# Gated attention: the next tile's low-rank transposition right behind the sums of decays, its gates' product one group sooner, and the sampled decays' sums in one bank

## The chip, the core and the metric

The kernel runs on one core of one Trainium2 chip. The metric is the device time of one launch in microseconds (us), lower is better. Besides the engines' own names, PE is TensorE, DVE is VectorE, ACT is ScalarE, POOL is GpSimd and SP is SyncE, whose queue issues the DMAs.

## The reference

One layer of a decoder: 2048 prompt tokens and 64 sampled tokens pass an input projection, sliding-window attention and gated linear attention side by side, an output projection and an MLP. The change touches the gated linear attention alone. Cut to that part, for 4 heads with keys of 64 and values of 128:

```python
log_a = jax.nn.log_sigmoid(glr @ w_gk2 + b_gk) / 16.0      # glr: 16 columns of the projection, the low-rank gate
b = cumsum(log_a) within a chunk                           # sums of decays
k_rel = exp(where(causal, b_t - b_s, -inf)) * k_s
o = (q_t . k_rel) v_s  +  (q * exp(b)) S                   # inside the chunk, and from the state
S = exp(b_last) * S + (k * exp(b_last - b))^T v            # the state that is carried on
out = rms_norm(o, g_gla) * silu(gr)
```

## The kernel before

The program runs in stages: attention, then the gated attention, then the output projection and the MLP. In the stage of the gated attention (some 430 us of the span) the 2048 prompt tokens are 16 tiles of 128 (`NB = 16`). Tile 16 (`i == NB`) is the 64 sampled tokens, whose own recurrence `gla_sample` is woven in between as `side`.

Tensor work of two kinds is interleaved on PE by hand. The *filling* is the generator `products()`: the input projections of tiles 16, 2, 3, ... 15 (tiles 0 and 1 were projected before), each in four chunks of columns in the order `G_ORDER = (3, 0, 1, 2)`, 24 products a chunk. Chunk 3 holds the 16 low-rank columns. The *recurrence* is `gla(i)`, a generator that yields the number of filling products to put behind its step. For a tile it issues:

1. `qk_T` (tile `gqk`): transposed queries and keys, then 38 filling products (`G_FILL[0]`) and the transposition `ogT` of the previous tile's output, whose copy out on ACT is `mo`, L1046.
2. `es`: the sums of decays from a position to the tile's end, two products into a bank of kind "d". ACT takes their exponential into `kd` (L1077). Then the output gate (`gate`, tile `sg`), the levels of decays, and 14 filling products.
3. Four groups of products `gm` (levels 0 and 1, 2 and 3, 4 and 5, then 6), 9 filling products between them. Behind each group stands one step of `decayed(i + 1)`, the preparation of the next tile: behind the first group `pg`, the transposition of the 16 low-rank columns, which DVE copies to `glrT` (L934); behind the second `z`, their product with the gate's weights, from which ACT and DVE make the logarithms `zt` (L940 to L943); behind the third `tT`, their transposition, copied to `before` (L1058), from which the levels of the next tile are summed (`level_sums`, L998 to L1003).
4. `ds`, 13 filling products, `o` (the output) and `finish_out` up to its yield.

Accumulators are banks by kind: kinds "a", "b" and "c" have two buffers each, "d" and "e" one. `gqk`, `es`, `pg`, `z` and `ds` all use the one bank "d", so each must wait until what the one before left there has been read. Projections take the two "a" in turn.

Engines run their instructions in the order in which the framework placed them. On PE that is the order of the code; on DVE and ACT the framework's scheduler mixes the steps, so one moved step can move others.

## Time and profile before

| what | value |
|---|---|
| median of 3 runs | 2268.26 us (2267.26 to 2268.97) |
| the profiled execution | 2265.7 us, its span 2263.9 us |
| mean granted TensorE clock | 0.993 |
| PE busy in the span | 2200.4 us (97%) |
| DVE, ACT, POOL busy in the span | 1620.4, 1203.7, 271.1 us |
| stage of the gated attention, 342 to 770 us: PE, DVE, ACT busy | 412.5, 358.6, 216.8 us of 428.0 |

The span runs from the first to the last instruction; 1.8 us lie around it. A row of the timeline gives start, length, engine, line, instruction, output<-inputs and count, and in brackets the time that the engine sat idle before it and what ended it. The small matmuls of PE overlap: a projection product is listed with some 0.35 us but starts 0.18 us after the one before. Almost all tensor instructions are listed under L140, a helper's line, so they are told apart by the tile that they write.

### The profile page before, as it was taken

What the parts mean: (1) busy time and instruction counts of PE and PEld (TensorE: products, weight loads), DVE (VectorE), ACT (ScalarE), POOL (GpSimd) and SP (SyncE); (2) the same over time, 40 slices, a digit from 0 to 9 for tenths busy, and PEclk for the clock granted to TensorE, in tenths of its full rate; (3) what the DMA queues carried; (4) which work ended last, traced back from release to release, by engine and by line L of the source; (5) the groups of instructions that cost most, each with busy time, mean ns of one, the idle gap of its engine ahead of it and who ended that gap; (6) DMA issues with size and microseconds to landing.
All of it is one profiled execution on the core that took longest, in us unless ns stands there. A gap on an engine that the chain in (4) does not pass through costs nothing.

```text
span 2263.9 us, 34089 instructions
## 1 busy us (share of the span) xinstructions
PE 2200.4 (97%) x11800; PEld 1879.6 (83%) x11800; DVE 1620.4 (72%) x3365; ACT 1203.7 (53%) x2498; POOL 271.1 (12%) x426
## 2 busy tenths in 40 slices
PE   8999999999999999999999999999999999999997
PEld 7888888889988788878888878888888888888886
DVE  5888878888888776687767787878544645755557
ACT  5777764445555444555555655555444444554445
POOL 2566412112121110000000000000000000000000
PEclk9999999999999999999999999999999999999999
DMA  7344222121112455865555666666655755866665
GB/s 235 119 140 143 96 88 77 58 73 52 62 52 66 144 190 182 274 212 206 183 186 201 251 219 213 228 245 229 226 184 178 228 175 185 279 226 216 223 194 197
DMA packets 229938, 392.65 MB, mean 173 GB/s; under 512 B 23057, under 2 KB 137638, under 8 KB 225782
## 3 DMA queue, kind: packets, MB, share of 16 engines
q1 hardware_dynamic: 229766, 390.48, 51.3%
q8 instruction: 93, 1.52, 0.3%
q14 instruction: 79, 0.65, 0.1%
HBM read 255.61 MB, written 135.86 MB: 173 GB/s over the span
## 4 chain that ended last, share of the span: by engine, by line
PE 70%; DVE 17%; ACT 6%; issue 3%; DMA 3%; POOL 1%; SPq 0%; DVEq 0%; ACTq 0%; POOLq 0%
PE dn L140 23%; PE uc L140 7%; PE ua L140 7%; PE gproj L140 7%; PE out L1266 6%; PE ud L140 3%; PE ue L140 3%; PE ub L140 3%; DVE s L140 2%; PE proj L140 2%; DVE AT L1009 1%; PE sam L140 1%; PE dsam L140 1%; PE out L140 1%; DVE pl L140 1%
## 5 line engine op out<-in xcount | busy, mean ns | idle before, releaser
L140 PE MATMUL dn<-ot,os 128*128 128x512 f32 x2688 | 623.6, 390 | 3.8 <-DVE ot L140 1.9
L140 PEld LDWEIGHTS dn<-ot,os 128*128 128x128 f32 x2688 | 503.9, 188 | 112.9 <-DVE ot L140 5.4
L140 DVE TENSOR_TENSOR os<-os 128x512 fp32r<-128x512 f32 x224 | 154.9, 691 | 228.4 <-ACT os L140 228.0
L140 ACT ACTIVATE os<-os 128x512 fp32r<-128x512 f32 x224 | 141.4, 631 | 280.9 <-DMA os<-s_d 233.0
L140 PE MATMUL gproj<-wg,gx 128*128 128x384 f32 (+1 forms) x1408 | 279.4, 348 | 1.9 <-ACT s_dec L612 1.6
L140 PEld LDWEIGHTS gproj<-wg,gx 128*128 128x128 f32 x1408 | 246.8, 191 | 12.4 <-issue 10.1
L140 ACT ACTIVATE st<-st 128x512 f32<-128x512 f32 x225 | 142.1, 632 | 135.3 <-DVE st L140 131.2
L140 PE MATMUL uc<-H,s 128*128 128x512 f32 x744 | 180.4, 392 | 3.4 <-ACT st L140 3.4
L140 PE MATMUL ua<-H,w 128*128 128x512 f32 x744 | 179.2, 390 | 0.6 <-ACT st L140 0.6
L140 PEld LDWEIGHTS uc<-H,s 128*128 128x128 f32 x744 | 140.7, 189 | 33.2 <-ACT st L140 3.9
L140 PEld LDWEIGHTS ua<-H,w 128*128 128x128 f32 x744 | 138.7, 188 | 28.9 <-ACT st L140 0.8
L216 POOL TENSOR_TENSOR frs<-rs_v,half 128x1 f32<-128x1 f32 (+1 forms) x13 | 8.8, 680 | 1235.0 <-DVE rs_v L140 1235.0
L140 DVE TENSOR_TENSOR st<-st 128x512 f32<-128x512 f32 x160 | 110.5, 692 | 61.9 <-ACT st L140 58.7
L1266 PE MATMUL out<-wo,mt 128*128 128x512 f32 x608 | 141.5, 391 | 0.0
L1266 PEld LDWEIGHTS out<-wo,mt 128*128 128x128 f32 x608 | 113.2, 188 | 22.9
L140 DVE TENSOR_TENSOR ot<-ot 128x512 fp32r<-128x512 f32 x128 | 88.4, 690 | 13.9 <-ACT ot L140 13.4
L140 ACT ACTIVATE s<-t 128x1024 fp32r<-128x1024 f32 x62 | 65.8, 1061 | 58.1 <-PE ue L140 24.6
L140 PE MATMUL proj<-wa_hi,xh 128*128 128x384 f32 (+1 forms) x272 | 95.7, 355 | 0.9 <-ACT wa_hi L140 0.6
L140 PE MATMUL proj<-wa_lo,xh 128*128 128x384 f32 (+1 forms) x272 | 94.3, 351 | 0.0
L140 PE MATMUL proj<-wa_hi,xl 128*128 128x384 f32 (+1 forms) x272 | 93.3, 347 | 0.0
L140 DVE TENSOR_TENSOR s<-t,s 128x1024 fp32r<-128x1024 f32 x62 | 76.0, 1226 | 21.7 <-ACT s L140 18.6
L140 ACT ACTIVATE ot<-ot 128x512 fp32r<-128x512 f32 x128 | 80.8, 631 | 19.6 <-DMA ot<-t_d 18.0
(407 smaller groups left out, 4107.9 us busy)
## 6 DMA issues: line engine op xcount, KB each, us to landing
os<-s_d SPq DMA_DIRECT2D x224, 256.0 KB, 2.8
s_d<-st SPq DMA_DIRECT2D x31, 1792.0 KB, 8.4
raw<-in_w_up SPq DMA_DIRECT2D x64, 512.0 KB, 5.7
ot<-t_d SPq DMA_DIRECT2D x128, 256.0 KB, 3.3
rt<-in_w_down SPq DMA_DIRECT2D x96, 256.0 KB, 3.0
t<-in_w_down SPq DMA_DIRECT2D x64, 256.0 KB, 3.3
t_d<-t SPq DMA_DIRECT2D x32, 512.0 KB, 6.9
gx<-xt_d SPq DMA_DIRECT2D x28, 512.0 KB, 4.1
```

What stands on the lines that cost most here:

```text
L140: ins = call(*a, **k)
L216: nc.gpsimd.tensor_tensor(out, v[:n], e, op=ALU.pow)
L1009: nc.vector.copy_predicated(dst, m, gm.rearrange("p h (m b) -> p h m b", b=b))
L1266: te.matmul(p_, x, w[:, cc], start=k + u == 0, stop=k == KT - 1 and u == len(products) - 1)
```

## The change

Four edits:

1. The steps of `decayed(i + 1)` are started right behind `es` of tile `i`, if chunk 3 of the next tile has been projected by then (`ahead`). `pg` so stands between `es` and the 14 filling products, and its next step, `z`, behind the first group of `gm` instead of the second. Behind the second group then stands nothing, and `tT` stays behind the third. By the order of the built program `ahead` holds in tiles 0 to 12; in tiles 13 and 14 the steps stand where they stood.
2. The projection's chunk 1 of the sampled tokens (tile 16) is summed in bank "e" instead of "a".
3. The sampled tokens' sums of decays for both pairs of heads go into one bank, and one exponential takes them instead of two.
4. `decayed` fetches its projection itself.

```diff
-            p_ = bank([P, 512], "a", f"gproj_{i}_{c}")
+            p_ = bank([P, 512], "ae"[(i, c) == (NB, G_ORDER[2])], f"gproj_{i}_{c}")
...
     def gla(i, gp, og=iter(())):
...
+        following = decayed(i + 1) if i < NB - 1 else iter(())
         next(og, None)
...
         ex = nc.scalar.activation(kd, e_, AF.Exp, scale=1.0 / 16)
         nc.gpsimd.tensor_tensor(kd, kd, gp[:, 256:512], op=ALU.mult)
+        ahead = (i + 1, 3) in projected
+        if ahead:
+            next(following, None)
         with tc.issue_after(ex.ins):
             sg = gate(i, gp, P)
...
-        following = decayed(i + 1, gps[i + 1]) if i < NB - 1 else iter(())
...
-            next(following, None)
+            if not (ahead and l0 == 2):
+                next(following, None)
...
+        e_ = bank([P, 2, (SL + 1) * NS], "b", "se")
         for g in range(2):
-            e_ = bank([P, (SL + 1) * NS], "b", f"se_{g}")
-            te.matmul(e_, lh[:NS, g * P : (g + 1) * P], slev, start=True, stop=False)
-            te.matmul(e_, ll[:NS, g * P : (g + 1) * P], slev, start=False, stop=True)
-            nc.scalar.activation(s_dec[:, g].rearrange("p l t -> p (l t)"), e_, AF.Exp, scale=1.0 / 16)
+            te.matmul(e_[:, g], lh[:NS, g * P : (g + 1) * P], slev, start=True, stop=False)
+            te.matmul(e_[:, g], ll[:NS, g * P : (g + 1) * P], slev, start=False, stop=True)
+        nc.scalar.activation(s_dec.rearrange("p g l t -> p g (l t)"), e_, AF.Exp, scale=1.0 / 16)
```

The first place is PE in tile 6, between the sums of decays and the second group. `gproj` are filling products. Before:

```order
L140 MATMUL es_6891<-lh_4955,c_suf 128x256
L140 MATMUL es_6891<-ll_4957,c_suf 128x256
L140 MATMUL gproj_1_6879<-wg_1_4344,gx_7_6496 128x384
...
L140 MATMUL gm_0_6969<-XQ,qk_4950 64x2x32 x4
L140 MATMUL gm_0_6969<-XQ,XK 64x2x32 x4
L140 MATMUL pg_6978<-ident,gp_6851 16x128
...
L140 MATMUL gm_2_6996<-XQ,XK 64x2x32 x8
L140 MATMUL z_7005<-wgk,glrT_4935 128x256
```

and in the change:

```order
L140 MATMUL es_6889<-lh_4955,c_suf 128x256
L140 MATMUL es_6889<-ll_4957,c_suf 128x256
L140 MATMUL pg_6894<-ident,gp_6849 16x128
L140 MATMUL gproj_1_6877<-wg_1_4344,gx_7_6494 128x384
...
L140 MATMUL gm_0_6970<-XQ,qk_4950 64x2x32 x4
L140 MATMUL gm_0_6970<-XQ,XK 64x2x32 x4
L140 MATMUL z_6979<-wgk,glrT_4935 128x256
...
L140 MATMUL gm_2_7002<-XQ,XK 64x2x32 x8
```

`pg` moved ahead of the 14 filling products and of the first group, directly behind `es`; `z` moved ahead of 9 filling products and of the second group.

The second place is DVE in tile 9. The names: `before` and L1003 are the sums of the levels, the one written 128x2x64 is the last; `XK` and `XQ` are keys and queries times their decays, `rs_v` and `og` belong to the previous tile's output. Before:

```order
L971 COPY qk_4951<-gqk_7653 128x2x128
L1002 TENSOR_TENSOR after_4949<-after_4949,before_4948 128x4x32
...
L214 TENSOR_SCALAR rs_v<-ossq_7639 128x4
...
L1031 SCALAR_TENSOR_TENSOR og_4939<-o_7632,ors_7645,sg_4943 128x128 x4
...
L1003 TENSOR_TENSOR before_4948<-before_4948 128x4x32
...
L1003 TENSOR_TENSOR before_4948<-before_4948 128x2x64
```

and in the change:

```order
L1003 TENSOR_TENSOR before_4948<-before_4948 128x4x32
L1017 COPY_PREDICATED AT<-dmsk,dg_7722 128x512
L971 COPY qk_4951<-gqk_7651 128x2x128
L1003 TENSOR_TENSOR before_4948<-before_4948 128x2x64
...
L214 TENSOR_SCALAR rs_v<-ossq_7637 128x4
...
L1031 SCALAR_TENSOR_TENSOR og_4939<-o_7630,ors_7643,sg_4943 128x128 x4
```

The last two sums moved from behind `og` to ahead of it. So it is in tiles 3 to 8 before and in tiles 2 to 11 and 13 in the change; in tiles 1, 2 and 9 to 14 before, and in tiles 1, 12 and 14 in the change, the last sum stands behind `og`.

The third place is DVE in tile 6, around the copy of `pg` and the logarithms. Before:

```order
L1090 TENSOR_TENSOR qd_4945<-qk_4950,dec_4947 128x256
L956 SCALAR_TENSOR_TENSOR sg_4943<-gp_6574,sg_4943 128x512
L1009 COPY_PREDICATED AT<-c_1527,gm_0_6969 64x4x32
L934 COPY glrT_4935<-pg_6978 16x128
...
L1009 COPY_PREDICATED AT<-c_1527,gm_2_6996 64x4x4x8 x2
L943 SCALAR_TENSOR_TENSOR zt_4952<-z_7005,zt_4952 128x256
```

and in the change:

```order
L1093 TENSOR_TENSOR qd_4945<-qk_4950,dec_4947 128x256
L934 COPY glrT_4935<-pg_6894 16x128
L956 SCALAR_TENSOR_TENSOR sg_4943<-gp_6572,sg_4943 128x512
L1009 COPY_PREDICATED AT<-c_1527,gm_0_6970 64x4x32 x2
L1009 COPY_PREDICATED AT<-c_1527,gm_0_6970 64x4x16x2 x2
L943 SCALAR_TENSOR_TENSOR zt_4952<-z_6979,zt_4952 128x256
```

The copy moved ahead of the gate and of the first group's copies, and the logarithms' last step ahead of the second group's.

## The prediction

> **What bounds the kernel now.** I read the page first: PE is busy 97% of the span, DVE 72%, ACT 53%. The change touches only the stage of the gated attention, so I then asked for that stage's waits of PE. A row names who waits, for whom, the sum in us, how often, and the longest.

> ```profile
> PE z L140 <- DVE glrT L934: 4.8, 7, 2.1
> PE tT L140 <- DVE zt L943: 3.1, 3, 1.4
> PE gm L140 <- DVE AT L1009: 2.7, 2, 2.4
> PE gproj L140 <- ACT s_dec L612: 1.6, 1, 1.6
> PE se L140 <- ACT s_qk L972: 1.1, 1, 1.1
> PE pg L140 <- ACT kd L1077: 0.6, 2, 0.3
> ```

> Some 14 us of waits in a stage of 428 us: PE is the bound almost everywhere, and the change aims at four of these six rows. Even if all of them went, the kernel would gain 0.6%. Any new wait on PE, on the other hand, is paid in full. So I cut the stage into tiles, from the second `es` product of one tile to that of the next. The columns are the stretch, its length, and PE's busy time in it (count, clock and DMA follow).

> ```profile
> 477.68:504.65 26.97, 25.23 (x197) 1.00 0.34 104
> 504.65:528.02 23.37, 23.37 (x182) 1.00 0.17 57
> 528.02:551.41 23.39, 23.39 (x181) 1.00 0.17 58
> ...
> 598.29:622.08 23.79, 23.45 (x182) 1.00 0.17 57
> 622.08:646.64 24.56, 23.58 (x181) 1.00 0.15 54
> 646.64:670.56 23.92, 23.52 (x182) 1.00 0.16 57
> 670.56:695.07 24.51, 23.61 (x181) 1.00 0.16 54
> 695.07:719.44 24.37, 23.56 (x181) 1.00 0.15 42
> ```

> The first row is tile 4. Tiles 5 and 6 are full: 23.37 us of work in 23.37 us. Tiles 9 to 13 lose 0.42, 1.19, 0.55, 1.14 and 1.00 us against that, 4.3 us together.

> **Part 1: `pg` right behind `es`.** Both use the one bank "d", so `pg` must wait until ACT has read the sums of decays (`kd`, L1077). Before, 14 filling products and a group lay between them. Tile 6, PE and then ACT:

> ```profile
> 528.02 0.27 PE L140 MATMUL es<-ll,c_suf 128*128 128x256 f32 x1
> 528.13 2.59 PE L140 MATMUL gproj<-wg,gx 128*128 128x384 f32 x14
> ...
> 531.27 0.28 PE L140 MATMUL pg<-ident,gp 128*16 128x128 f32 x1
> 531.30 1.83 PE L140 MATMUL gproj<-wg,gx 128*128 128x384 f32 x9
> ```

> ```profile
> 528.10 0.60 ACT L1046 ACTIVATE mo<-ogT 128x512 f32<-128x512 f32 x1 [0.55 <-PE ogT L140]
> 528.59 0.38 ACT L1077 ACTIVATE kd<-es 128x256 f32<-128x256 f32 x1
> ```

> `kd` cannot start at once: ACT first copies `ogT`, which PE finished just ahead of `es`. It ends at 528.97, when PE before had been in the filling for 0.84 us. What a waiting `pg` does to PE is seen in tile 10, where ACT was so late that `pg` waited in spite of its distance:

> ```profile
> 624.47 0.42 ACT L1088 ACTIVATE dec<-before 128x256 f32<-128x256 f32 x1 [4.18 <-DVE before L1003]
> ...
> 625.27 0.38 ACT L1077 ACTIVATE kd<-es 128x256 f32<-128x256 f32 x1
> ```

> ```profile
> 625.70 0.28 PE L140 MATMUL pg<-ident,gp 128*16 128x128 f32 x1 [0.30 <-ACT kd L1077]
> 625.74 1.83 PE L140 MATMUL gproj<-wg,gx 128*128 128x384 f32 x9
> ...
> 628.73 0.69 PE L140 MATMUL z<-wgk,glrT 17*128 17x256 f32 x2 [0.54 <-DVE glrT L934]
> ```

> PE stood still until 0.05 us after the end of `kd` (625.65), and the filling behind went on 0.04 later: nothing overtakes a waiting `pg`. So in tile 6 the filling would start at 528.97 + 0.09 = 529.06 instead of 528.13, less 0.03 for the slot of `pg` that is no longer spent at 531.27: 0.90 us lost. Queued behind it are the 14 filling products, `gm`, and with `gm` DVE. A tile of this kind has no idle time on PE that could give it back. The DVE order puts the last sums ahead of `og` in tiles 2 to 11 of the change, the pattern of tile 6 (`kd` on time): 10 x 0.90 = 9.0 us. (Bounds 0.7, if the copy `mo` starts sooner, to 1.0.)

> Tile 12 has its last sum behind `og`, as tiles 9 to 14 had before. There ACT waits for that sum (the 4.18 us above) with `mo` and `kd` queued behind. Where the filling began behind `es` in tiles 9 and 12, and what ended the wait:

> ```profile
> 598.40 2.59 PE L140 MATMUL gproj<-wg,gx 128*128 128x384 f32 x14
> ...
> 670.67 2.59 PE L140 MATMUL gproj<-wg,gx 128*128 128x384 f32 x14
> ...
> 674.13 0.28 PE L140 MATMUL pg<-ident,gp 128*16 128x128 f32 x1 [0.25 <-ACT kd L1077]
> ```

> ```profile
> 600.30 0.38 ACT L1077 ACTIVATE kd<-es 128x256 f32<-128x256 f32 x1
> ```

> As in tile 9 (the first of its row to be late, as tile 12 will be) the loss is 600.68 + 0.09 - 598.40 - 0.03 = 2.3 us, as in tile 12 674.13 - 670.67 = 3.5. I take the middle, 2.9.

> Tiles 0 and 1 are different: there the sampled tokens' work keeps DVE nearly full (first row: stretch, length, DVE busy), and PE's end of tile 0 waits for DVE's `og`.

> ```profile
> 358.43:385.85 27.42, 25.37 (x72) 0.94 0.06 20
> 384.72 1.13 DVE L1031 SCALAR_TENSOR_TENSOR og<-o,ors,sg 128x128 f32<-128x128 f32 x4 [0.72 <-POOL ors L216]
> ```

> ```profile
> 386.24 0.60 PE L140 MATMUL ogT<-ident,og 128*128 128x128 f32 x4
> 386.91 1.38 PE L140 MATMUL gproj<-wg,gx 128*128 128x384 f32 x7
> ```

> ```profile
> 390.45 0.38 ACT L1077 ACTIVATE kd<-es 128x256 f32<-128x256 f32 x1
> ```

> In tile 0 PE's waits of 1.6 (`s_dec`) and 2.1 us (the longest of `z`) do go, by part 2 and the earlier copy, but `ogT` comes only 0.39 us after `og` ends (385.85): PE arrives sooner and waits there. I take 0, bounds -1 and +1. In tile 1 `pg` must wait for `kd` at 390.83: 390.92 - 386.91 - 0.03 = 4.0 us lost.

> **The clock** bears on tile 1. Granted TensorE clock is the column after PE's, DVE's, ACT's and POOL's busy times; PE's comes first behind the length.

> ```profile
> 365.19:368.60 3.41, 1.32 (x20) 0.84 (x18) 3.36 (x8) 0.90 (x2) 1.40 (x2) 1.00 0.17 68
> 368.60:372.01 3.41, 3.41 (x11) 2.82 (x9) 3.20 (x9) 2.35 (x5) 0.00 (x0) 0.50 0.01 2
> ...
> 399.32:402.73 3.41, 3.41 (x25) 3.27 (x26) 3.09 (x13) 0.56 (x2) 0.00 (x0) 0.50 0.01 4
> 488.07:491.48 3.41, 2.08 (x13) 1.81 (x15) 3.22 (x12) 0.79 (x2) 0.00 (x0) 1.00 0.03 6
> ```

> After a stretch of 3.41 us with PE busy 1.32 the next 3.41 ran at half clock, which costs 1.7 us; a stretch with 2.08 busy had no such result. So waits of 0.9 us are safe, tile 1's 4.0 us may halve the clock, tile 12's are at the edge. [...]

> Tile 1 also wins: the wait of `se` (1.1), one of `z` (I count 0.56, as in tile 10) and, without those, perhaps the half clock at 399.32 (1.7). 4.0 - 3.4 = +0.6 if all come, +4.0 if none; DVE, which has nothing to do until `gm` comes later, holds a part back. I take +1.5.

> **Part 2: what the earlier steps and the banks save elsewhere.** With the copy `glrT` ahead of the first group's copies on DVE and `z` 9 products sooner, `zt` is ready long before `tT`, which stays in place. In tile 4 two waits go:

> ```profile
> 487.29 0.69 PE L140 MATMUL gm<-XQ,XK 128*64 128x64 f32 x16 [0.31 <-DVE AT L1009]
> 489.40 0.44 PE L140 MATMUL tT<-ident,zt 128*128 128x128 f32 x2 [1.43 <-DVE zt L943]
> ```

> -1.7 us. In tiles 9 to 13 the last sums are on time (9 to 11, 13) or their waits merge into the long one at `pg` (12): all 4.3 us go. The wait of `tT` in tile 14 (3.1 - 1.43 - 0.34, the 0.34 being tile 9's idle time) stays, since its steps are not moved. One exponential less on ACT and the `e` bank beyond tile 0 cost and save nothing on PE: ACT is half idle.

> **Sum.** Tile 0: 0; tile 1: +1.5; tiles 2 to 11: +9.0; tile 12: +2.9; tile 4: -1.7; tiles 9 to 13: -4.3. Together +7.4 us, on the profiled 2265.7 us: 2273.1. That execution lies 2.6 us below the median of the runs, 2268.26, against which the change will be timed: 2275.7, 0.33% slower. Its own bounds: low ends (-1, 0.6, 7.0, 2.3, with all savings and 3 us more) give about +1, high ends (1, 4.0 and 1.7 of clock, 10, 3.5 and 1.7 of clock, half the savings) +19: 2269 to 2287.

> **The rivals.**

> *The new wait costs nothing* (faster). If PE went on with the filling while `pg` waits, 9.0, 2.9 and 4.0 us would fall away, leaving the savings: -1.7 - 4.3 - 3.4 = -9.4, 2259. It decides at a loss per tile below some 0.3 us. For it: the weight loads run apart from the matmuls. Against it: the two waits of `pg` before, with filling queued behind. [...] 13%, with other gains.

> *No change.* The stalls give DVE and ACT a rest of 0.9 us a tile, and more waits go than I count: tile 14's 1.3, the 2.4 of `gm` in tile 15 with the half clock behind it (1.7), half of tile 0's 3.7. 7.4 - 7.2 = 0. For it: DVE is nearly as full as PE in these tiles. Against it: tiles 14 and 15 keep their order, and 0.9 us on each of ten full tiles is hard to hide. 27%.

> *Much slower.* `kd` stays late in tiles 9 to 11 too, as before, because of a lateness that carries over; then each stalls some 3 us instead of 0.9, +6, and tiles 1 and 12 lose the clock: +3.4. 2285. Against it: the order of DVE there is that of tiles 5 to 8. 12%.

> **How the numbers follow.** 48% for the forecast, of which a tenth may still fall within 0.2% (4.5 us, about what a measurement of this kernel can tell from no change), as a tenth of the second rival may fall above it. Slower: 0.43 + 0.12 + 0.03 = 0.58; same: 0.05 + 0.24 = 0.29; faster: 0.13. The range leaves out the first rival and the far end of the last: 2265 to 2284.

> **What the changed profile would show.** `pg` waiting for ACT `kd` in 13 tiles, over 12 us in all, at the top of PE's waits; clean tiles of 24.3 instead of 23.4 us; `z` on `glrT`, `tT` on `zt` (but for tile 14) and `gproj` on `s_dec` gone; a wait of `ogT` on `og` at the end of tile 0; the longest `pg` wait in tile 1, the next in tile 12. I am wrong if `kd` ends right with `es` there, or if PE idles less than 0.3 us at `pg` in tile 6.

## The result, and the profile after

The change made the kernel slower: 2284.8 us median (2281.8 to 2291.3) against 2268.5 (2264.1 to 2269.2), ratio 1.0079, interval 1.0067 to 1.0091. That is +16.4 us where +7.4 was forecast; the sign was right, the size was wrong, and the time lies just above the range. Measured once more in another job (`after_again`, below) it was 2283.1 against 2269.0, ratio 1.0064 (1.0051 to 1.0078). The profiled execution of the change took 2281.8 us against 2265.7, a difference of 16.1.

PE's waits in the stage of the gated attention, in the columns of before:

```profile
PE pg L140 <- ACT kd L1078: 14.2, 13, 3.1
PE gm L140 <- DVE AT L1009: 5.8, 3, 2.8
PE tT L140 <- DVE zt L943: 1.4, 1, 1.4
...
PE ogT L140 <- DVE og L1031: 0.2, 1, 0.2
```

The row of `pg` grew from 0.6 to 14.2 us and leads the list; `z`, `se` and the wait for `s_dec` are gone. So far this is the forecast. But all rows of this view together grew from 15.0 to 22.9 us, and the kernel lost 16. The rest is seen when the stage is cut into tiles, as for the kernel before (stretch, length, PE busy, count, clock, DMA). First tiles 0 to 3 of before, then tiles 0 to 6, 9 and 11 to 13 of the change:

```profile
358.43:386.80 28.37, 24.69 (x179) 0.94 0.05 19
386.80:417.38 30.58, 28.87 (x205) 0.94 0.13 44
417.38:448.27 30.89, 30.89 (x237) 0.94 0.24 78
448.27:477.68 29.41, 29.03 (x222) 0.94 0.12 45
```

```profile
360.02:389.53 29.51, 25.82 (x178) 0.88 0.05 19
389.53:425.36 35.83, 32.74 (x205) 0.81 0.11 37
425.36:455.95 30.59, 29.86 (x237) 1.00 0.25 79
455.95:484.98 29.03, 27.86 (x221) 1.00 0.12 46
484.98:511.93 26.95, 25.64 (x197) 1.00 0.35 104
511.93:536.31 24.38, 23.66 (x181) 1.00 0.16 55
536.31:560.71 24.40, 23.67 (x181) 1.00 0.16 55
609.57:633.95 24.38, 23.65 (x181) 1.00 0.16 55
...
658.39:682.79 24.40, 23.67 (x181) 1.00 0.15 56
682.79:710.67 27.88, 24.94 (x182) 0.94 0.14 48
710.67:734.04 23.37, 23.37 (x182) 1.00 0.16 43
```

| tiles | forecast, us | measured, us |
|---|---|---|
| 0 | 0 | +1.1 |
| 1 | +1.5 | +5.3 |
| 2 and 3 | +1.8 | -0.7 |
| 4 | -0.8 | 0.0 |
| 5 to 8 | +3.6 | +4.0 |
| 9 to 11 | +0.5 | +0.9 |
| 12 | +1.8 | +3.4 |
| 13 | -1.0 | -1.0 |
| 14 | 0 | -0.1 |
| sum | +7.4 | +12.9 |
| ahead of tile 0, behind tile 14 | 0 | +3.2 |

The clean tiles came out nearly as worked out: 24.4 us, 1.0 more each (24.3 and 0.90 in the forecast). PE in tile 6 of the change:

```profile
536.31 0.27 PE L140 MATMUL es<-ll,c_suf 128*128 128x256 f32 x1
537.32 0.28 PE L140 MATMUL pg<-ident,gp 128*16 128x128 f32 x1 [0.73 <-ACT kd L1078]
537.35 2.71 PE L140 MATMUL gproj<-wg,gx 128*128 128x384 f32 x14
```

The filling starts 1.04 us behind `es`, where it had started 0.11 behind it; less the 0.03 of the slot that `pg` no longer takes, that is the 0.90 of the forecast. The misses stand where the clock column is below 1: tile 1 (0.81) and tile 12 (0.94), and in the other direction tiles 2 and 3, where before had 0.94 and the change 1.00. Two long waits of `pg` stand ahead of these stretches, in tiles 1 and 12, and a new wait in tile 0:

```profile
372.21 1.12 PE L140 MATMUL gm<-XQ,XK 128*64 128x64 f32 x16 [2.83 <-DVE AT L1009]
...
392.90 0.38 PE L140 MATMUL pg<-ident,gp 128*16 128x128 f32 x1 [3.09 <-ACT kd L1078]
...
686.00 0.38 PE L140 MATMUL pg<-ident,gp 128*16 128x128 f32 x1 [2.94 <-ACT kd L1078]
```

The stretches of 3.41 us around the wait in tile 1, then those around the one in tile 12, same columns:

```profile
388.36:391.77 3.41, 1.45 (x11) 1.00 0.00 0
391.77:395.18 3.41, 2.28 (x8) 0.50 0.20 77
395.18:398.60 3.42, 3.42 (x11) 0.50 0.00 0
398.60:402.01 3.41, 3.41 (x22) 0.50 0.00 0
402.01:405.42 3.41, 3.41 (x14) 0.50 0.00 0
...
681.91:685.32 3.41, 1.16 (x9) 1.00 0.00 0
685.32:688.73 3.41, 2.73 (x9) 0.50 0.20 77
```

In tile 1 the clock stayed at half for four steps of 3.41 us, in three of which PE was busy from end to end. I had priced one step, 1.7 us, and only in the upper bound.

### The profile page after: what moved, and what is told of

It is laid out like the page before. It is cut to its first block, busy times and chain, and to the rows that moved or that the text cites. A ratio compares the mean times of both kernels' runs of the same rounds, so it can differ in the third digit from the quotient of the medians.

```text
span 2280.0 us, 34104 instructions
## 1 busy us (share of the span) xinstructions
PE 2208.5 (97%) x11800; PEld 1884.8 (83%) x11800; DVE 1629.8 (71%) x3365; ACT 1205.6 (53%) x2497; POOL 273.8 (12%) x426
## 4 chain that ended last, share of the span: by engine, by line
PE 75%; DVE 13%; ACT 6%; issue 3%; DMA 2%; POOL 1%; SPq 0%; DVEq 0%; ACTq 0%; POOLq 0%
PE dn L140 25%; PE gproj L140 9%; PE uc L140 7%; PE ua L140 7%; PE out L1270 5%; PE ud L140 3%; PE ue L140 3%; PE ub L140 3%; DVE s L140 2%; PE proj L140 2%; PE sam L140 1%; PE gm L140 1%; PE dsam L140 1%; PE out L140 1%; DVE pl L140 1%
## 5 line engine op out<-in xcount | busy, mean ns | idle before, releaser
L140 PE MATMUL dn<-ot,os 128*128 128x512 f32 x2688 | 624.3, 390 | 3.2 <-DVE ot L140 1.6
L140 PEld LDWEIGHTS dn<-ot,os 128*128 128x128 f32 x2688 | 505.1, 188 | 111.8 <-DVE ot L140 4.6
L140 DVE TENSOR_TENSOR os<-os 128x512 fp32r<-128x512 f32 x224 | 154.8, 691 | 226.9 <-ACT os L140 226.4
L140 ACT ACTIVATE os<-os 128x512 fp32r<-128x512 f32 x224 | 141.4, 631 | 280.9 <-DMA os<-s_d 227.4
L140 PE MATMUL gproj<-wg,gx 128*128 128x384 f32 (+1 forms) x1408 | 282.9, 351 | 0.9 <-DMA gx<-xt_d 0.9
L140 PEld LDWEIGHTS gproj<-wg,gx 128*128 128x128 f32 x1408 | 248.9, 192 | 12.6 <-issue 10.1
L140 ACT ACTIVATE st<-st 128x512 f32<-128x512 f32 x225 | 142.0, 632 | 135.1 <-DVE st L140 131.0
L140 PE MATMUL uc<-H,s 128*128 128x512 f32 x744 | 180.5, 392 | 3.5 <-ACT st L140 3.5
L140 PE MATMUL ua<-H,w 128*128 128x512 f32 x744 | 179.3, 390 | 0.8 <-ACT st L140 0.8
L140 PEld LDWEIGHTS uc<-H,s 128*128 128x128 f32 x744 | 140.7, 189 | 33.2 <-ACT st L140 3.9
L140 PEld LDWEIGHTS ua<-H,w 128*128 128x128 f32 x744 | 138.7, 188 | 29.3 <-ACT st L140 1.0
L216 POOL TENSOR_TENSOR frs<-rs_v,half 128x1 f32<-128x1 f32 (+1 forms) x13 | 9.8, 753 | 1234.7 <-DVE rs_v L140 1234.7
L140 DVE TENSOR_TENSOR st<-st 128x512 f32<-128x512 f32 x160 | 110.4, 692 | 61.8 <-ACT st L140 58.6
L140 DVE TENSOR_TENSOR ot<-ot 128x512 fp32r<-128x512 f32 x128 | 88.3, 690 | 12.9 <-ACT ot L140 11.9
L140 PE MATMUL proj<-wa_hi,xh 128*128 128x384 f32 (+1 forms) x272 | 95.9, 356 | 0.9 <-ACT wa_hi L140 0.6
L140 ACT ACTIVATE s<-t 128x1024 fp32r<-128x1024 f32 x62 | 65.8, 1061 | 58.1 <-PE ue L140 24.6
L140 PE MATMUL proj<-wa_lo,xh 128*128 128x384 f32 (+1 forms) x272 | 94.6, 352 | 0.0
L140 PE MATMUL proj<-wa_hi,xl 128*128 128x384 f32 (+1 forms) x272 | 93.6, 348 | 0.0
L140 DVE TENSOR_TENSOR s<-t,s 128x1024 fp32r<-128x1024 f32 x62 | 76.0, 1226 | 21.7 <-ACT s L140 18.6
L140 ACT ACTIVATE ot<-ot 128x512 fp32r<-128x512 f32 x128 | 80.8, 631 | 19.9 <-DMA ot<-t_d 13.5
```

Source lines behind the costliest of these rows:

```text
L140: ins = call(*a, **k)
L216: nc.gpsimd.tensor_tensor(out, v[:n], e, op=ALU.pow)
```

## The experiments

All ratios are to the kernel before, run on the same chip in the same job.

**Which part of the change costs.** Part 1 undone:

```diff
-        ahead = (i + 1, 3) in projected
+        ahead = False
```

> The changed kernel with part 1 undone (the steps of decayed stand where they stood before; the sampled sums in one bank, the e bank of chunk 1 and the shape of decayed stay). Theory (the whole loss is in the moved steps): only the wait of se for the sampled queries (1.1 us in tile 1) goes, so 2266 to 2269 us, ratio to before 0.999 to 1.000. Rival (the banks cost a part of the 9 us that I had not forecast): 2271 us or more, ratio 1.0015 or above.

Measured: 2268.8 us, ratio 1.0004 (0.9995 to 1.0012). The banks alone change nothing that can be told. In the trace the wait of `se` is gone, and one of `tT` (1.17 us) stands in tile 1 instead. The counterpart is part 1 with the banks of before:

> Part 1 of the change alone: the early steps, with the banks of before (two banks and two exponentials for the sampled sums, chunk 1 in bank a). Theory (the banks do nothing): 2282 to 2288 us, as the whole change. Rival (the e bank or the one exponential costs something that shows only with the early steps): 2280 or less.

Measured: 2279.2 us, ratio 1.0050 (1.0037 to 1.0062). That is most of the loss but below the 2282 that I had expected, and it fell on the rival's side. So both were run together:

> The changed kernel itself, beside part 1 alone on the same chip. Theory (how long the half clock lasts behind the long wait in tile 1 hangs on where the 3.41 us steps of the clock fall, and the two measurements drew other shares of that): the two kernels within 2 us of each other, both 2279 to 2286. Rival (the banks cost some 5 us once the steps are early): 2283 to 2287 here, part 1 alone 2277 to 2281.

> Part 1 alone once more, beside the changed kernel on the same chip. Theory (no cost of the banks): within 2 us of the changed kernel. Rival: 4 to 6 us faster than it.

Measured: the change 2283.1, ratio 1.0064 (1.0051 to 1.0078); part 1 alone 2279.7, ratio 1.0049 (1.0036 to 1.0062). The medians are 3.4 us apart, between the two theories, and the intervals overlap. By the medians of the two jobs part 1 carries two thirds to three quarters of the loss. Whether the banks add 3 us to it is not settled.

**Is it the clock?** The wait in tiles 1 and 12 filled with products that nobody reads:

```diff
+        if i in (1, 12):
+            busy = bank([P, 256], "c", f"busy_{i}")
+            for _ in range(26 if i == 1 else 25):
+                te.matmul(busy, suf, lh, start=True, stop=True)
         if ahead:
             next(following, None)
```

> The changed kernel with 26 products of the shape of es into a free bank ahead of pg in tile 1 and 25 in tile 12; their output is not used. They last about as long as PE waited there for kd (3.1 and 2.9 us), so the wait is as long as before but PE is busy in it. Theory (half clock behind the long waits costs about 6 us in tile 1 and 1.7 in tile 12): no half clock there, tile 1 from 35.8 to about 30 us, tile 12 from 27.9 to 26.3, total 2276 to 2280 us. Rival (the clock is only a bystander, DVE bounds these tiles): 2284 to 2287 us.

Measured: 2277.4 us, ratio 1.0043 (1.0029 to 1.0058). PE in tile 1, and the step of the clock behind the extra products:

```profile
387.64 3.25 PE L140 MATMUL busy<-lh,c_suf 128*128 128x256 f32 x26
391.22 0.28 PE L140 MATMUL pg<-ident,gp 128*16 128x128 f32 x1 [0.33 <-ACT kd L1078]
```

```profile
389.27:392.69 3.42, 3.09 (x23) 1.00 0.20 77
392.69:396.10 3.41, 3.41 (x29) 1.00 0.02 5
```

`pg` starts no sooner behind `es` than it did in the change (3.7 us here, 3.4 there), no step at half clock is left in the two tiles, and tile 1 takes 31.8 us instead of 35.8 (the theory had said about 30; PE waits 0.89 us for `og` at its end) and tile 12 26.6 instead of 27.9. Those 4.0 and 1.3 us are the price of the half clock, apart from that of the wait. The medians, 2277.4 against 2284.8 and 2283.1 in other jobs, agree: the kernel got faster by doing more.

**The same wait in another tile.** The early steps in tiles 2 to 11 only:

```diff
-        ahead = (i + 1, 3) in projected
+        ahead = 2 <= i <= 11
```

> The changed kernel with the early steps in tiles 2 to 11 alone; tiles 0, 1 and 12 keep the old order. Theory (the surplus over the forecast came from the long waits of pg in tiles 1 and 12 with the half clock behind them, and from tile 0): tiles 5 to 8 still take 24.4 us, no pg wait above 1 us, total 2284.8 - 5.3 - 3.4 - 1.1 = 2275, range 2271 to 2278. Rival (the early steps cost their surplus everywhere, or elsewhere): 2280 or more.

Measured: 2280.2 us, ratio 1.0058 (1.0045 to 1.0071); 5 us above the theory. Tiles 0, 1 and 12 came back (28.4, 28.9, 24.2 us), but with the change cut out of tile 1 DVE's last sum stood behind `og` in tile 2, `kd` was late there, and the long wait had moved. PE and the clock's steps in tile 2:

```profile
418.86 0.28 PE L140 MATMUL pg<-ident,gp 128*16 128x128 f32 x1 [3.13 <-ACT kd L1078]
...
422.95 3.59 PE L140 MATMUL s_oe<-s_qd,s 128*128 128x16 f32 x16
```

```profile
415.92:419.33 3.41, 0.47 (x3) 1.00 0.00 0
419.33:422.75 3.42, 3.42 (x14) 0.50 0.20 77
...
436.40:439.81 3.41, 3.41 (x26) 0.50 0.00 0
439.81:443.23 3.42, 3.42 (x37) 1.00 0.72 217
```

Six steps at half clock, 20.5 us, with PE fully busy in each: tile 2 took 11 us more than before (41.9 against 30.9), of which the wait itself is 3.1. In these steps stand the sampled tokens' small products (`s_oe` writes 16 columns) between few filling products. Without tile 2:

> As mid_tiles, but the early steps in tiles 3 to 11 alone, so that tile 2, too, keeps the old order. In mid_tiles the wait of pg moved into tile 2 (3.1 us there) and the clock was at half for 20.5 us behind it; tile 2 took 41.9 us. Theory (the wait is cheap, the half clock behind it is dear): tile 2 back at 31 to 33 us, no pg wait above 1 us, total 2280.2 - 9.9 = 2270, range 2267 to 2273. Rival (the half clock there has another cause, such as the sampled tokens' small products alone): tile 2 stays above 36 us, 2275 or more.

Measured: 2272.1 us, ratio 1.0019 (1.0011 to 1.0027), tile 2 at 32.9 us, no wait of `pg` above 0.8. As forecast. Two steps at half clock remain in tile 2 with no long wait ahead of them (`banks_only` has two there as well, before one), so the wait brought four of the six, and tile 2 is 9.0 us shorter without it. This run is the early step without any long wait: nine tiles, 4.6 us slower.

**Is the wait for the bank the whole price?** `pg` in a bank of kind "b":

```diff
-        pg = bank([P, P], kind, f"pg_{i}")
+        pg = bank([P, P], "b", f"pg_{i}")
```

> The changed kernel, all steps where the change puts them, but pg goes into one of the two banks of kind b, so it has no reason to wait for kd; z stays in d. Theory (the wait for the bank is the whole price of the early step): no pg wait in tiles 2 to 11, these tiles 23.4 us, tile 1 without its 3.1 us, total 2259 to 2265 us, faster than before. Rival (the position costs by itself, through DVE's earlier copy): tiles above 24 us and 2270 us or more.

Measured: 2272.4 us, ratio 1.0024 (1.0013 to 1.0035): still slower than before, and my theory missed. PE in tile 5, whose length hardly moved (24.36 us):

```profile
508.21 0.27 PE L140 MATMUL pg<-ident,gp 128*16 128x128 f32 x1
...
512.41 0.67 PE L140 MATMUL z<-wgk,glrT 17*128 17x256 f32 x2 [0.87 <-DVE glrT L934]
```

The wait for `kd` is gone and one for DVE's copy `glrT` has come, of about the same size. The copy ends some 4.2 us behind `es` in this tile of both programs; the second early step, `z`, only found it ready in the change because `pg` had held PE up. In tiles 7 and 8 `z` waits as well (0.58 and 0.82 us; all three tiles take 24.4), there for a copy that itself ends 0.5 to 0.7 us later behind `es` than in the change; tile 6 has no such wait and takes 23.5. The rest of the loss stands elsewhere: tile 2 takes 36.4 us (30.9 before), with four steps at half clock, and in tile 12 `pg` waits 2.15 us for its operand. With `z` back in its old place:

```diff
-            if not (ahead and l0 == 2):
+            if not (ahead and l0 == 0):
                 next(following, None)
```

> As b_bank (pg behind es in a bank of kind b, so without a wait for kd), but z in its old place behind the second group. In b_bank the wait of pg was gone and tiles 5, 7 and 8 still took 24.4 us, because z behind the first group waited 0.6 to 0.9 us for DVE's copy glrT. Theory (both early steps run into an engine that is not ready, each for about 0.9 us, and the second hides behind the first): tiles 5 to 8 back at 23.4 us, total 2262 to 2268. Rival (the early copy on DVE costs by itself): tiles 5 to 8 above 24 us and 2272 or more.

Measured: 2268.1 us, ratio 1.0000 (0.9992 to 1.0008), just above the theory's 2268; tiles 5 to 8 are back at 23.5 to 23.6 us. Both early steps must be freed of their wait before the loss goes, and then nothing is won: PE had been full in these tiles before. Restricted to tiles 3 to 12:

> As z_late_b in tiles 3 to 12 alone; the tiles with the sampled tokens' work keep the order of before, and pg is in a bank of kind b only where it is early. Theory: no wait of pg, none of z in tiles 3 to 12, the rest as with the banks alone: 2268 - about 3 = 2265, range 2261 to 2267, faster than before. Rival (those waits only move on to tT or gm): 2267 to 2270, no change.

Measured: 2272.2 us, ratio 1.0017 (1.0009 to 1.0026); a miss. Tile 12 takes 26.2 us as in z_late_b, since there `pg` waits 2.55 us for its own operand, which ACT copies out of the projection's bank (`gp`, L617), and in tiles 10 and 11 `tT` waits (0.91 and 0.22 us) where `z` did. The median is 4 us above that of z_late_b. In the profiled executions, 8.7 us apart, tiles 0 and 2, which keep the old order here, and tile 3 took 4.3 us more together, and there are nine steps at half clock ahead of the last 10 us against three; what set them off is not shown.

The opposite: `z` late and `pg` early in bank "d". In this program DVE's last sum stands behind `og` again in tiles 9 to 14:

> The changed kernel (pg behind es in bank d, waiting for kd) with z in its old place. In this order of the program DVE's last sum stands behind og again in tiles 9 to 14. Theory (pg's wait alone costs what kd is late, and above some 3 us the clock too): tiles 5 to 8 still 24.4 us, tiles 9 to 12 stall about 2 to 3 us each, some at half clock behind it: tiles of 26 to 30 us, total 2292, range 2285 to 2305. Rival (z was the dear one of the two): tiles 5 to 8 at 23.4 us, total 2275 or less.

Measured: 2297.1 us, ratio 1.0125 (1.0112 to 1.0138), with tiles 5 to 8 at 24.4 to 24.7 us, as the theory had it. The row of `pg`, and tiles 9 and 10:

```profile
PE pg L140 <- ACT kd L1078: 21.7, 13, 3.6
```

```profile
613.10:640.42 27.32, 25.15 (x181) 0.94 0.15 49
640.42:668.33 27.91, 25.20 (x182) 0.94 0.14 48
```

Each of the tiles 9 to 12 pays its wait (2.2 to 2.9 us) and one step at half clock behind it, as tile 12 of the change does. It confirms the forecast's third rival as a mechanism; the change escaped it only because its order on DVE was the good one.

**Is the order of DVE the root?** The sums of the levels are written ahead of the previous tile's `og`, in the changed kernel:

```diff
+        dec = next(decs)
+        for l, b in enumerate(LEVELS):
+            level_sums(before, after, dec, l, b)
         next(og, None)
         qk = qk_T(i, gp, P)
-        dec = next(decs)
...
-            level_sums(before, after, dec, l, b)
             leveled(XK if l else None, XQ, dec, qk, l, b, P)
```

> The changed kernel, with the sums of the levels (level_sums) written ahead of the previous tile's og, so that DVE has its last sum ahead of og in tiles 1 to 14; no order on PE changes. Theory (the long waits of pg come from kd standing on ACT behind that last sum, and the half clock from the long waits): no pg wait above 1.1 us, tile 1 from 35.8 to 30 to 32 us, tile 12 from 27.9 to 24.4, tiles 5 to 11 still 24.4, total 2276, range 2273 to 2279. Rival (tile 1 is bound by the sampled tokens' work on DVE, whatever kd does): tile 1 above 34 us, 2280 or more.

Measured: 2269.2 us, ratio 1.0005 (0.9996 to 1.0014), 7 us better than the theory and below its range; tile 0, which the theory left out, took 27.7 us, 1.8 less than in the change. The row of `pg`, then tiles 1 and 12:

```profile
PE pg L140 <- ACT kd L1080: 9.3, 13, 0.8
```

```profile
386.92:418.11 31.19, 30.46 (x206) 0.89 0.13 43
...
675.04:699.48 24.44, 23.71 (x182) 1.00 0.16 54
```

No wait of `pg` above 0.8 us, tile 1 in its range, tile 12 clean, tiles 5 to 11 still 24.4. Two steps at half clock are left in tile 1 (0.89 in its row): in the step ahead of them fall two shorter waits, 1.22 us of `ogT` and 0.73 of `pg`. The long waits came from DVE's order, by way of `kd`. The same edit without the early steps:

> The kernel with the banks alone (steps of decayed where they were before), with the same sums written ahead of og. Theory (the 4.3 us that tiles 9 to 13 lost before came from the late last sum, not from the place of z): tiles 9 to 13 at 23.4 us, total 2268.5 - 5 = 2263, range 2259 to 2266, faster than before. Rival (og late on DVE makes ogT late on PE instead): waits of ogT, 2267 or more.

Measured: 2256.2 us, ratio 0.9949 (0.9936 to 0.9961), faster than both kernels. Tiles 10 and 12:

```profile
617.82:641.24 23.42, 23.42 (x181) 1.00 0.17 57
...
664.65:688.08 23.43, 23.43 (x182) 1.00 0.16 57
```

All tiles from 5 to 13 are full. This wins the 4.3 us that I had credited to the change, and shows what they hung on: the place of DVE's last sum, which the change moved as a side effect. With the early steps the same program takes 13 us more in this job, 8.0 of them in tiles 5 to 12, 1.0 each. Whether the banks have a part in the gain:

> The kernel before with nothing changed but the sums of the levels written ahead of the previous tile's og. Theory (the whole gain of 12 us comes from the order of DVE, the banks give nothing): 2255 to 2259 us. Rival (the banks' parts, wait of se in tile 1 above all, give some of it): 2260 or more.

> sums_first once more (the sums ahead of og, both banks, no early steps), beside its parts on one chip. Theory: 2255 to 2259 us again. Rival (the 9 us between it and sums_alone were a draw): 2260 or more.

> The sums ahead of og and the sampled sums in one bank, chunk 1 in bank a as before. If the wait of se (1.7 us in sums_alone, with a step at half clock behind it) is what the banks save: 2257 to 2261. If the e bank is what saves it: 2263 to 2266.

> The sums ahead of og and chunk 1 of the sampled tokens in bank e, the sampled sums in two banks as before. If the wait of se is what the banks save: 2262 to 2266. If the e bank is what saves it (the wait for s_dec in tile 0, 1.1 us in sums_alone): 2257 to 2261.

Measured: without banks 2265.0, ratio 0.9975 (0.9963 to 0.9987), and in another job with both 2261.0 (0.9962, 0.9950 to 0.9975), with the sampled sums' bank alone 2258.9 (0.9952, 0.9940 to 0.9965), with the "e" bank alone 2263.0 (0.9969, 0.9958 to 0.9981). Without banks the time fell on the rival's side, and so did the repetition: the 2256.2 did not come again, one kernel drew medians 4.8 us apart in two jobs. The two parts of the banks came out as they would if the wait of `se` were what is saved. By the interval of `sums_alone` the order of the sums is worth at least 3 us by itself; that the sampled sums' bank adds some, by the wait of `se`, is likely from the medians, but the intervals overlap.

## Why the prediction was right and wrong

**What bounds the kernel: right.** PE pays every new wait in full: where nothing else differs (after_sums beside sums_first), each of the tiles 5 to 12 is 1.0 us longer.

**`pg` behind `es`, 0.90 us a tile: right.** In tiles 2 to 11 `pg` waited 0.72 to 0.77, the start of the filling in tile 6 moved by just the 0.90, and the clean tiles grew by 0.97 to 1.01; the term for tiles 5 to 8 was 3.6 and measured 4.0. One thing was missing in the reasoning though not in the number: b_bank shows that in three of these four tiles the second early step costs about as much without it.

**Tiles 1 and 12: the step that failed.** "I take +1.5" for tile 1 (measured +5.3) and the "middle, 2.9" for tile 12 (measured 27.88 - 23.37 = 4.5 over a full tile). The waits were sized well enough: a loss of 4.0 and 2.9 us was worked out, and 3.3 and 3.1 are measured in the same way, from `es` to the filling (PE waited 3.09 and 2.94). PE's idle time, length less busy time in the rows above, grew by 1.4 us in tile 1 and 2.0 in tile 12, near the forecast terms of +1.5 and +1.8. The clock behind the waits was what I had wrong: I wrote that tile 1's wait "may halve the clock" and put tile 12 "at the edge", priced each at one step of 1.7 us in the upper bound alone, and the sum had nothing for either. The half clock lasted four steps in tile 1, one in tile 12, and PE's busy time grew by 3.9 and 1.3 us for it. junk shows this as a cause: with `pg` no sooner and PE busy, 4.0 and 1.3 us go. The miss as a whole is of this size too: ahead of their last 10 us the profiled execution of the change has twelve steps at half clock and that of before seven. Five more, at 1.7 us where PE is busy, are 8.5 us, and the profiled difference of 16.1 lies 8.7 above the forecast.

The step's source was a single row: one step at half clock behind a gap, with PE full in it. I read "one step" as the length of a penalty. In the runs it lasted one to six steps, and a PE that was busy throughout did not end it: mid_tiles has six steps in a row at half clock in which PE's row shows 3.41 busy of 3.41, so busy time in the row is not what counts here. What does go with it in the traces of before and of the change is how many columns the products moved, as the last section shows: small products keep PE's row busy and move few (16 of `s_oe` fill 1.96 us in tile 2 of before and move 256). It was not tried by an edit of its own.

**Tile 0: the waits turned into others.** `s_dec` and `z` (3.7 us) went, as forecast, and 0.86 of `pg` and 2.83 of `gm` came, 3.7 us. I had named `ogT` as the next to be late; it was `gm`, which stands earlier and had to wait until DVE's copies (`AT`) had read its bank. PE's idle time in the tile stayed at 3.7 us; the +1.1 is a second step at half clock.

**Tiles 2 and 3: better by luck.** Before lost a step of the clock in each (0.94), the change in neither. I had not counted on that, in either direction; it hid 2.5 us of the miss.

**The savings.** Tiles 9 to 13: right in sum, and sums_first shows why. Tile 4: wrong. The wait of `tT` went, but that of `gm` stayed (0.34), those of `pg` (0.73) and `ogT` (0.25) came, and the tile kept its length.

**Outside the stage: +3.2.** The program ahead of tile 0 is the same, yet it took 1.6 us more in the profiled execution: a gap near 37 us cost two steps at half clock instead of one. Among the kernels here that went either way, so I count it as chance; the 1.6 behind tile 14 stands beside one more step at half clock in the later stages.

**The rivals.** Against "costs nothing": every clean tile. The weight loads do run beside the matmuls (before, PEld was busy for 1879.6 us and PE for 2200.4 in the span of 2263.9), but the filling began only behind the waiting `pg` (537.35 behind 537.32 in tile 6 of the change). Against "no change": the stalls gave DVE no rest that helped PE. "Much slower" came nearest in time (2285), but by its second clause alone, the clock in tiles 1 and 12; `kd` was on time in tiles 9 to 11. One sum was wrong as well: the low ends of the bounds add up to -0.1 us, not to about +1.

## What to carry to other kernels

Where the tensor engine is full, moving a step earlier in its order won nothing here even with its bank free, and it cost a wait wherever the operand or the bank was not ready at the new place; look up when the bank's last reader ends, on its own engine, and what that one is queued behind. A stall of some 1.9 us or more within one 3.41 us step of the clock was followed by half clock each time in the traces of before and of the change (8 of 8 steps), so price it with the clock behind it. How long the clock stays down goes with what follows the stall: in these runs it was back after one step of mostly filling products (tile 12 of the change), and stayed down through stretches with many small ones (four steps in tile 1 of the change, six in tile 2 of mid_tiles). And ask which moved instruction on another engine made a tile better: here the useful part of the change was an accident of DVE's order, and written on purpose it gave 0.25%, with the banks 0.4 to 0.5%.

## What the runs showed of the hardware

```profile
393.18 0.28 PE L140 MATMUL pg<-ident,gp 128*16 128x128 f32 x1 [3.22 <-ACT kd L1078]
```

```profile
388.38:391.79 3.41, 1.57 (x12) 1.00 0.00 0
391.79:395.20 3.41, 2.02 (x11) 1.00 0.20 77
395.20:398.62 3.42, 3.42 (x30) 1.00 0.00 0
```

The clock never dropped there, and the tile took 30.5 us; in its first run the same kernel took 33.7 with two steps at half clock, the change 35.8. In this tile that is 3 us between two runs of one kernel. Of the steps at full clock from 60 to 2250 us in the executions of before and of the change, 8 had PE busy for 1.50 us or less, and each was followed by half clock; of the 5 between 1.51 and 2.10 one was; above that it happened three times, in tiles 1 to 3 of before, among the sampled tokens' products. So a stall of about 1.9 us within one step was dear each time, and a shorter one seldom. A single profile of such a kernel is one draw, and a few us between two of them mean little.

**A full step can lose the clock too.** Before, in tile 2, PE was busy throughout, with the sampled tokens' products of 16 columns in it, and the clock dropped behind it:

```profile
419.84 1.96 PE L140 MATMUL s_oe<-s_qd,s 128*128 128x16 f32 x16
```

```profile
419.80:423.21 3.41, 3.41 (x30) 1.00 0.20 79
423.21:426.63 3.41, 3.41 (x25) 0.50 0.00 0
```

**Columns moved tell the clock better than busy time.** The rows give each product's size, so the columns that PE moves in a step can be added up, each product's spread from its start to the next one's (or to its own end, if that comes first) and counted by the share that its weights have of the 128x128 of a filling product: a filling product of 128x384 counts 384, `s_oe` 16. From 340 to 800 us the executions of before and of the change have 268 steps, at either clock. All 9 that moved fewer than 2400 such columns were followed by half clock, 3 of them with PE busy throughout; all 252 that moved 3000 or more were followed by full clock; of the 7 between, four were followed by half. Spread to the listed ends instead, one step of 3090 was followed by half too, so no sharp limit is shown. In tile 2 of before the step from 419.80 moved 2206 and the next 2968, and the clock fell and came back. This is a count over two traces, not an experiment, but it fits the stalls, the long half clock in tile 1 of the change (2394, 2479, 2581 and 1683 columns, then 2901) and the full steps that lost the clock alike.
